# Router decisions from logits, a finer first gather, slot weights one batch at a time, and 28 unread products on TensorE

## The chip, the cores and the metric

The kernel runs on one core of one Trainium2 chip. The metric is the device time of one execution in microseconds (us). TensorE (PE; its weight loads are PEld) multiplies, VectorE (DVE) does elementwise work and reductions, ScalarE (ACT) evaluates functions and copies, GpSimd (POOL) helps, and SyncE (SP) issues the weight transfers on its DMA queue.

## The reference

One block of another kind comes first, then two layers of this form on 256 tokens of width 1024. The change concerns only the second half of each layer, a mixture of experts (MoE) with 4 groups of 8 experts:

```python
g_prob = softmax(t @ w_group + b_group)            # 4 groups
p_sel, g_idx = top_k(g_prob, 1)
e_in = the 8 expert logits of the chosen group
e_prob = softmax(e_in)
w_k, i_k = top_k(e_prob, 2);  w_k = w_k / sum(w_k)
combine = p_sel * one_hot(g_idx) * inner            # inner holds w_k at i_k
hid = silu(t @ w_gate[g]) * (t @ w_up[g]) * combine
x = x + sum over experts of hid @ w_down[g]
```

## The kernel before, in words

All matrices come from one packed array, in units of 1 MB (128 partitions x 2048 floats). `Stream` issues one transfer for each unit on SP's queue (L309) into a ring of buffers called `raw`; a unit's transfer is issued when the unit that held its buffer has been read. Before each MoE stage other pools are lent to the ring, so that it has 8 + 4 + 5 = 17 buffers.

The end of the mixers (`mixers2`) adds the output product to `x` for the token halves i = 0 and 1, and `r_logits` runs the router for a half in steps: sum of squares, transposes of `x` (`xT`, copied to `qh`), logits (`lg`, 8 products with 36 columns, then `L` on VectorE), the first group with the largest logit (`oh`), the chosen group's 8 logits (`el`), their largest (`emx`), an exponential on ScalarE with its sum (`pe`, `es`), a division, the two largest (`MAX` into `m8`, `MATCH_REPLACE`), the marks of the two chosen experts (`ci`), and `sel`, the 32 marks of a token. A product with a triangular matrix (`rank`) counts earlier tokens with the same expert, and `place` is the token's slot. `weave` and a list scheduler settle the order of the instructions; each engine then works its list strictly in order.

`route` compares `place` with the slot numbers: `OH[token, expert*32 + slot]` is 1 where the token sits. It makes the 256 columns of the first 8 experts (L1625, 128x256) and then the other 768, for each half. `gather` multiplies `x` by `OH` in row blocks k of 128 features: for a pair of batches (8 experts, 256 slots) and a k there are two products, one for each half i, and VectorE moves the result with a gain to `XT`. Before the change a step of `gather` handles two row blocks in one PSUM tile `gat`.

`experts` loops over NB = 8 batches of 4 experts. A batch has 8 units for gate and up (`gu`, one unit for each k: 4 products on 32 columns of the array) and 4 for down (`y`). After each unit `st.load()` lets SP issue the next transfer. `slots` multiplies all of `OH` by `ci` (`comb`, 16 products with 9 columns) for the weight and scale of every slot, and `tot` counts tokens for an overflow branch that is normally not taken. `turn_slots` transposes `OH` (`ohT`) for the way back (`sc`). All PE products have the helper's line L431.

The lines of the loop that set the order in the first batch:

```python
            for k in range(8):
                if b == 0 and k in (0, 2, 4):
                    next(first)
                w = unit()
                for j in range(4):
                    s.mm(q[j * SL:j * SL + SL, :], XT[b % 2][:, k, j * SL:j * SL + SL], w[:, j, :], k == 0, k == 7)
                st.load()
```

Of the kernel before, what the change touches and what calls it, by code (L numbers as in the profile page):

```python
# [16 lines left out]
T = 256  # L17
# [8 lines left out]
NB = 8  # L26
# [239 lines left out]
def run(*gens):  # L266
    for g in gens:
        for _ in g:
            pass
# [135 lines left out]
class KB:  # L405
# [754 lines left out]
    def mixers2(s, l, p):  # L1160
        nc, st = s.nc, s.st
        v = s.v = {}
        g = s.g("n2")[:, 8 * l:8 * l + 8]
        wr = s.g("router")[:, 288 * l:288 * l + 288].rearrange("p (k f) -> p k f", k=8)
        s.wr = s.p_ro.tile([128, 8, 36], F32, name="wr")
        nc.gpsimd.tensor_mul(s.wr, wr, g[:, :, None].to_broadcast([128, 8, 36]))
        for name, n in (("L", 36), ("r", 1), ("gt", 4), ("oh", 4), ("place", 32), ("psel", 1), ("ge", 4), ("gnx", 1), ("gmx", 2)):
            setattr(s, name, s.p_ro.tile([128, 2, n], F32, name=name))
        s.sel = s.p_ro.tile([128, 2, 32], F32, name="sel")
        s.ci = s.p_ro.tile([128, 2, 9], F32, name="ci")  # L1170
        xh = s.xnh = p.tile([128, 8, T], F32R, name="xnh")
# [24 lines left out]
        dense = s.m2_dense(l, pe)  # L1196
        weave((1.0, dense), (1.0, s.m2_stick(l, pe, dense)), (0.8, s.m2_mla(l, pe, (0, 1))))
        y = [[s.ps("wo", tag="y") for c in range(2)] for i in range(2)]
        m2 = s.m2_mla(l, pe, (2, 3))
        weave((1.0, s.m2_out(y, (6, 7, 4, 5))), (1.0, m2))  # L1200
        s.es_e.close()
        s.px = s.right(f"lx{l}")
        st.lend(s.px, "raw", s.E)
        U = [st.take() for k in range(4)]

        def last(i):
            for k in range(4):
                h, lo = U[k]
                mh, ml = s.m2_o(k)
                for c in range(2):  # L1210
                    s.mm3(y[i][c], mh[:, i * 128:i * 128 + 128], ml[:, i * 128:i * 128 + 128],
                          h[:, c * 512:c * 512 + 512], lo[:, c * 512:c * 512 + 512], False, k == 3)
                    yield 0.65

        run(last(0))
        weave((1.0, last(1)), (1.0, s.r_logits(l, p, 0, y[0])))
        st.done(4)
        st.lend(s.p_hl, "hl", s.S)
        run(s.r_logits(l, p, 1, y[1]))

    def right(s, name):

# [328 lines left out]
    def r_logits(s, l, p, i, y):  # L1551
# [27 lines left out]
        v.scalar_tensor_tensor(t, L[:, 0:4], mx[:, 0:1], s.c("first"), op0=OP.is_equal, op1=OP.mult)  # L1579
        v.tensor_reduce(mx[:, 1:2], t, axis=AX.X, op=OP.max)  # L1580
        v.tensor_scalar(oh, t, mx[:, 1:2], None, op0=OP.is_equal)

        v.tensor_scalar(s.gnx[:, i], mx[:, 0:1], -1.0, None, op0=OP.mult)
        nc.scalar.activation(s.ge[:, i], L[:, 0:4], AF.Exp, bias=s.gnx[:, i], accum_out=s.psel[:, i])
        yield 1.0


        def small(name, *shape):
            return s.p_ro.tile([128, *shape], F32, name=f"{name}{i}")

        em, el, emx, pe, es, m8, pr, w2 = (small(*n) for n in (("em", 4, 8), ("el", 8), ("emx", 1), ("pe", 16), ("es", 1), ("m8", 8), ("pr", 16), ("w2", 1)))
        v.tensor_mul(em, L[:, 4:36].rearrange("p (g e) -> p g e", g=4), oh[:, :, None].to_broadcast([128, 4, 8]))
        v.tensor_reduce(el, em.rearrange("p g e -> p e g"), axis=AX.X, op=OP.add)
        v.tensor_reduce(emx, el, axis=AX.X, op=OP.max, negate=True)
        nc.gpsimd.memset(pe, -1.0)
        nc.scalar.activation(pe[:, 0:8], el, AF.Exp, bias=emx, accum_out=es)
        yield 1.0
        v.reciprocal(es, es)
        v.tensor_scalar(pe[:, 0:8], pe[:, 0:8], es, None, op0=OP.mult)
        v.max(m8, pe[:, 0:8])  # L1600
        v.tensor_add(w2, m8[:, 0:1], m8[:, 1:2])
        v.memset(m8[:, 2:8], -1.0)
        v.match_replace(pr, m8, pe, -2.0)
        ci = s.ci[:, i]
        v.tensor_scalar(ci[:, 0:8], pr[:, 0:8], -2.0, None, op0=OP.is_equal)
        v.tensor_mul(s.sel[:, i].rearrange("p (g e) -> p g e", g=4), oh[:, :, None].to_broadcast([128, 4, 8]), ci[:, None, 0:8].to_broadcast([128, 4, 8]))
        yield 1.0

        q = s.ps("rank", tag="by"[i])
        s.mm(q[:, 0:32], s.c("lt"), s.sel[:, i], True, i == 0)  # L1610
# [4 lines left out]
        v.tensor_mul(w2, w2, s.psel[:, i])  # L1615
        v.reciprocal(w2, w2)
        v.scalar_tensor_tensor(ci[:, 0:8], ci[:, 0:8], w2, pe[:, 0:8], op0=OP.mult, op1=OP.mult)
        v.tensor_copy(ci[:, 8:9], s.r[:, i])

    def route(s, l, OH):  # L1620
        v = s.nc.vector
        for g0, g1 in ((0, 1), (1, 4)):
            for i in range(2):
                n = 8 * (g1 - g0)
                v.tensor_tensor(OH[:, i, g0 * 256:g1 * 256].rearrange("p (e s) -> p e s", s=SL), s.c("slot")[:, None, :].to_broadcast([128, n, SL]),  # L1625
                                s.place[:, i, g0 * 8:g1 * 8, None].to_broadcast([128, n, SL]), op=OP.is_equal)
        s.silu_set()

    def gather(s, l, XT, g, OH):

        gain = s.g("n2")[:, 8 * l:8 * l + 8]
        for k in range(0, 8, 2):
            q = s.ps("gat")
            for kk in range(2):
                d = slice((k + kk) * 128, (k + kk) * 128 + 128)
                for i in range(2):
                    s.mm(q[:, kk * 256:kk * 256 + 256], s.x[:, i, d], OH[:, i, g * 256:g * 256 + 256], kk == 0 and i == 0, i == 1)
            for j in range(2):
                s.nc.vector.tensor_tensor(XT[j][:, k:k + 2, :], q.rearrange("p (k j t) -> p k j t", k=2, j=2)[:, :, j], gain[:, k:k + 2, None].to_broadcast([128, 2, 128]), op=OP.mult)  # L1639
            yield  # L1640

    def slots(s, OH, comb):

        nc = s.nc
        v = nc.vector
        q = s.ps("comb")
        for b in range(NB):
            for i in range(2):
                s.mm(q[:, b * 9:b * 9 + 9], OH[:, i, b * 128:b * 128 + 128], s.ci[:, i, :], b == 0 and i == 0, i == 1)
        c9 = s.p_ro.tile([128, NB, 9], F32, name="c9")  # L1650
        v.tensor_copy(c9, q[:, :NB * 9].rearrange("p (b e) -> p b e", b=NB))
        c8 = c9[:, :, 0:8].rearrange("p (g h) e -> p g h e", h=2)
        v.tensor_mul(c8, c8, s.c("pick").rearrange("p (h e) -> p h e", h=2)[:, None].to_broadcast([128, 4, 2, 8]))
        v.tensor_reduce(comb[:, :, 0:1], c9[:, :, 0:8], axis=AX.X, op=OP.add)
        v.tensor_copy(comb[:, :, 1:2], c9[:, :, 8:9])
        v.tensor_mul(comb[:, :, 0:1], comb[:, :, 0:1], comb[:, :, 1:2])
        q = s.ps("tot")
        for i in range(2):
            s.mm(q[:, 0:32], s.one, s.sel[:, i], i == 0, i == 1)
# [13 lines left out]
    def experts(s, l, p, OH, OHT, comb):  # L1673
# [51 lines left out]
        for b in range(NB):  # L1725
# [1 line left out]
                es.enter_context(s.tc.manual_schedule(engines=_TAIL))  # L1727
            q = s.ps("gu")
            for k in range(8):
                if b == 0 and k in (0, 2, 4):  # L1730
                    next(first)
                w = unit()
                for j in range(4):
# [1 line left out]
                st.load()  # L1735
                if k == 1 and b:
                    hT = turned(hid)
                if k == 3:
                    if b == 0:
                        s.slots(OH, comb)  # L1740
                    if b % 2 == 0:
                        s.turn_slots(OH, OHT, b)
                    if b % 2 and b + 1 < NB:
                        nxt = tiles()
                        run(s.gather(l, nxt, b // 2 + 1, OH))
# [119 lines left out]
```

## Time and profile before

| | us |
|---|---|
| median of 3 runs (1229.9 to 1231.47) | 1230.11 |
| the profiled execution's own time | 1230.79 |
| its span, first to last instruction | 1229.0 |
| PE busy | 1112.7 (91%) |
| PEld / DVE / ACT / POOL busy | 824.7 / 566.2 / 462.6 / 127.9 |
| mean granted TensorE clock | 0.94 |

The profile divides the span into 40 slices of 30.7 us. The router and the start of the first MoE stage lie near 655 to 725 us, those of the second near 983 to 1040 us. A granted clock of 1.00 is 2.4 GHz and 0.50 is 1.2 GHz. A DMA share of 1.01 means that all 16 DMA engines were busy throughout.

### The profile page before, as it was taken

To read this page: it belongs to the slowest core of one execution; us is meant where nothing else is said; L and a number is where in the kernel's file an instruction comes from. 1 tells how busy PE (TensorE), PEld (TensorE's weight loads), DVE (VectorE), ACT (ScalarE), POOL (GpSimd) and SP (SyncE) were. 2 spreads that over 40 slices of the span, in tenths; PEclk is the share of its full clock that TensorE was granted. 3 is DMA by queue.
4 is the path that set the end of the run, shared out by engine and by line. 5 is a ranking of instruction groups with operands and counts; after the bars stand their busy time and mean duration, and the time that the engine had idled before them with its cause. 6 is when DMAs were issued, how large, how long until landed. Compare 5 with 4: busy or idle time off the path is not lost.

```text
span 1229.0 us, 18560 instructions
## 1 busy us (share of the span) xinstructions
PE 1112.7 (91%) x7474; PEld 824.7 (67%) x7474; DVE 566.2 (46%) x1121; ACT 462.6 (38%) x886; POOL 127.9 (10%) x143
## 2 busy tenths in 40 slices
PE   7999999999999999999998998867799989978665
PEld 7999999878789999998976623212198765313111
DVE  5555555669857555556865111100187552101002
ACT  6444444467646444445753010000177420110002
POOL 0222211000002221223120000000003000000000
PEclk9999999999999999999998899868889989988887
DMA  9754445653213545544428799999984389999996
GB/s 362 276 180 173 165 166 196 146 177 135 104 66 145 199 175 192 185 176 174 171 83 349 291 419 420 420 417 419 418 325 146 114 339 371 418 420 420 416 420 247
DMA packets 46469, 320.65 MB, mean 261 GB/s; under 512 B 5560, under 2 KB 5688, under 8 KB 9248
## 3 DMA queue, kind: packets, MB, share of 16 engines
q1 hardware_dynamic: 44640, 314.43, 65.0%
q0 software_dynamic: 1264, 4.26, 1.7%
q8 instruction: 62, 1.02, 0.3%
q10 hardware_dynamic: 464, 0.63, 0.1%
q14 instruction: 39, 0.32, 0.1%
HBM read 316.61 MB, written 2.69 MB: 260 GB/s over the span
## 4 chain that ended last, share of the span: by engine, by line
PE 67%; DMA 23%; DVE 6%; ACT 2%; issue 1%; SPq 0%; DVEq 0%; ACTq 0%
DMA raw<-in_weights_dram 22%; PE pg L431 11%; PE pu L431 10%; PE wo L431 6%; PE pd L431 5%; PE py L431 5%; PE gat L431 4%; PE gu L431 3%; PE sc L431 3%; PE qk L431 2%; PE y L431 2%; PE low L431 2%; PE po L431 2%; DVE whl L332 1%; PE qb L431 1%; PE iq L431 1%
## 5 line engine op out<-in xcount | busy, mean ns | idle before, releaser
L332 DVE TENSOR_TENSOR whl<-raw,whl 128x1024 fp32r<-128x1024 f32 (+2 forms) x211 | 261.1, 1239 | 153.7 <-ACT whl L331 153.6
L331 ACT CAST whl<-raw 128x1024 fp32r<-128x1024 f32 (+1 forms) x213 | 220.6, 1036 | 250.1 <-PE pu L431 53.1
L431 PE MATMUL gu<-raw,XT 128*32 128x512 f32 x1024 | 145.4, 670 | 42.1 <-DMA raw<-in_weights_dram 29.5
L431 PE MATMUL pg<-xh,whl 128*128 128x272 f32 (+1 forms) x704 | 137.5, 287 | 1.0 <-DVE gt L638 1.0
L431 PE MATMUL pu<-xh,whl 128*128 128x272 f32 (+1 forms) x704 | 136.2, 284 | 0.0
L431 PEld LDWEIGHTS pg<-xh,whl 128*128 128x128 f32 x704 | 113.1, 190 | 2.2 <-issue 1.2
L431 PEld LDWEIGHTS pu<-xh,whl 128*128 128x128 f32 x704 | 112.2, 188 | 0.0
L431 PEld LDWEIGHTS gu<-raw,XT 128*32 128x32 f32 x1024 | 26.2, 114 | 124.8 <-DMA raw<-in_weights_dram 67.7
L431 PE MATMUL pg<-xl,whl 128*128 128x272 f32 (+1 forms) x352 | 100.8, 286 | 0.0
L431 PE MATMUL pu<-xl,whl 128*128 128x272 f32 (+1 forms) x352 | 100.3, 285 | 0.0
L431 PE MATMUL y<-raw,hT 128*32 128x512 f32 x512 | 79.6, 707 | 17.3 <-DMA raw<-in_weights_dram 15.9
L1749 DVE SCALAR_TENSOR_TENSOR hid<-gu,comb,sg 128x256 f32<-128x256 f32 x16 | 7.7, 484 | 167.8 <-ACT sg L1747 167.8
L1747 ACT ACTIVATE sg<-gu,comb 128x256 f32<-128x256 f32 x16 | 7.6, 473 | 182.5 <-PE gu L431 182.5
L457 DVE TENSOR_TENSOR yl<-y,yh 128x512 fp32r<-128x512 f32 x32 | 22.1, 692 | 114.6 <-ACT yh L456 114.6
L431 PE MATMUL gat<-OH,x 128*128 128x256 f32 x256 | 71.1, 431 | 3.0 <-DVE OH L1625 3.0
L457 POOL TENSOR_TENSOR hl<-hid,hh 128x272 fp32r<-128x272 f32 (+1 forms) x44 | 57.7, 1310 | 123.8 <-ACT hh L456 123.7
L431 PEld LDWEIGHTS gat<-OH,x 128*128 128x128 f32 x256 | 52.8, 215 | 24.4 <-issue 11.7
L431 PEld LDWEIGHTS pg<-xl,whl 128*128 128x128 f32 x352 | 66.9, 190 | 0.8
L431 PE MATMUL pd<-hh,whl 128*128 128x272 f32 x352 | 66.9, 289 | 0.0
L431 PEld LDWEIGHTS pu<-xl,whl 128*128 128x128 f32 x352 | 66.2, 188 | 0.0
L456 ACT CAST yh<-y 128x512 fp32r<-128x512 f32 x32 | 18.7, 585 | 112.3 <-PE y L431 112.3
L1639 DVE TENSOR_TENSOR XT<-gat,sm 128x256 f32<-128x256 f32 x64 | 24.2, 420 | 76.7 <-PE gat L431 76.7
(413 smaller groups left out, 1984.8 us busy)
## 6 DMA issues: line engine op xcount, KB each, us to landing
raw<-in_weights_dram SPq DMA_DIRECT2D x290, 1024.0 KB, 15.4
raw<-in_weights_dram SPq DMA_DIRECT2D x6, 768.0 KB, 4.3
raw<-in_weights_dram SPq DMA_DIRECT2D x5, 512.0 KB, 7.6
dl<-line POOLq DMA_DIRECT2D x1, 1600.0 KB, 37.1
tb<-dl POOLq DMA_DIRECT2D x1, 1088.0 KB, 7.6
x<-in_x_dram SPq DMA_DIRECT2D x4, 256.0 KB, 5.0
c<-in_consts_dram POOLq DMA_DIRECT2D x1, 954.0 KB, 6.2
sm<-in_smalls_dram SPq DMA_DIRECT2D x1, 712.0 KB, 18.8
```

The lines of the kernel that those rows point to most:

```text
L331: s.kb.nc.scalar.copy(h[:, :n], raw)
L332: (s.kb.nc.gpsimd if s.spare is True or s.spare and j else s.kb.nc.vector).tensor_sub(l[:, :n], raw, h[:, :n].bitcast(F32))
L431: s.nc.tensor.matmul(out, l, r, start=start, stop=stop, skip_group_check=True)
L456: s.nc.scalar.copy(h, x)
L457: (s.nc.gpsimd if gpsimd else s.nc.vector).tensor_sub(l, x, h.bitcast(F32))
L1639: s.nc.vector.tensor_tensor(XT[j][:, k:k + 2, :], q.rearrange("p (k j t) -> p k j t", k=2, j=2)[:, :, j], gain[:, k:k + 2, None].to_broadc ...
L1747: nc.scalar.activation(sg, q[:, :256], AF.Silu, scale=comb[:, b, 1:2])
L1749: v.scalar_tensor_tensor(hid, q[:, 256:], comb[:, b, 0:1], sg, op0=OP.mult, op1=OP.mult)
```

## The change

Four things change in each of the two MoE layers. The two chosen experts are found from the logits `el` (padded to 16 with -3e38) and not from the exponentials; both exponentials of a half are issued later in the program, and a function `weights`, called in `route`, computes the weights of the chosen two. The first gather goes by single row blocks, one ahead of the loop and one before each `gu` of k = 0 to 6. `slots` runs for one batch at a time at k = 5, `turn_slots` at k = 5 of odd batches, and the count of tokens moves to batch 2 (`full`). Between the second half's logits and its `rank`, PE gets 28 products of 256 columns into a PSUM tile `idle` that nothing reads.

```diff
-        run(s.r_logits(l, p, 1, y[1]))
+        steps = s.r_logits(l, p, 1, y[1])
+        for n in range(4):
+            next(steps)
+
+        q = s.ps("idle")
+        for n in range(28):
+            s.mm(q[:, :T], s.ident_r, xh[:, 6, :])
+        run(steps)
...
-        nc.scalar.activation(s.ge[:, i], L[:, 0:4], AF.Exp, bias=s.gnx[:, i], accum_out=s.psel[:, i])
-        yield 1.0
...
-        v.tensor_reduce(el, em.rearrange("p g e -> p e g"), axis=AX.X, op=OP.add)
-        v.tensor_reduce(emx, el, axis=AX.X, op=OP.max, negate=True)
-        nc.gpsimd.memset(pe, -1.0)
-        nc.scalar.activation(pe[:, 0:8], el, AF.Exp, bias=emx, accum_out=es)
-        yield 1.0
-        v.reciprocal(es, es)
-        v.tensor_scalar(pe[:, 0:8], pe[:, 0:8], es, None, op0=OP.mult)
-        v.max(m8, pe[:, 0:8])
-        v.tensor_add(w2, m8[:, 0:1], m8[:, 1:2])
-        v.memset(m8[:, 2:8], -1.0)
-        v.match_replace(pr, m8, pe, -2.0)
+        v.tensor_reduce(el[:, 0:8], em.rearrange("p g e -> p e g"), axis=AX.X, op=OP.add)
+        v.max(m8, el[:, 0:8])
+        v.tensor_scalar(emx, m8[:, 0:1], -1.0, None, op0=OP.mult)
+        v.memset(m8[:, 2:8], -3.0e38)
+        v.match_replace(pr, m8, el, 3.0e38)
...
+        nc.scalar.activation(s.ge[:, i], L[:, 0:4], AF.Exp, bias=s.gnx[:, i], accum_out=s.psel[:, i])
+        nc.scalar.activation(pe, el[:, 0:8], AF.Exp, bias=emx, accum_out=es)
+
+        def weights():
+            v.reciprocal(es, es)
+            v.scalar_tensor_tensor(pe, pe, es, ci[:, 0:8], op0=OP.mult, op1=OP.mult)
+            v.tensor_reduce(w2, pe, axis=AX.X, op=OP.add)
+            v.tensor_mul(w2, w2, s.psel[:, i])
+            v.reciprocal(w2, w2)
+            v.tensor_scalar(ci[:, 0:8], pe, w2, None, op0=OP.mult)
+            v.tensor_copy(ci[:, 8:9], s.r[:, i])
...
         for g0, g1 in ((0, 1), (1, 4)):
+            if g0:
+                for f in s.weights:
+                    f()
...
-        for k in range(0, 8, 2):
+        n = 2 if g else 1
+        for k in range(0, 8, n):
...
-        for b in range(NB):
-            for i in range(2):
-                s.mm(q[:, b * 9:b * 9 + 9], OH[:, i, b * 128:b * 128 + 128], s.ci[:, i, :], b == 0 and i == 0, i == 1)
+        for i in range(2):
+            s.mm(q[:, 0:9], OH[:, i, b * 128:b * 128 + 128], s.ci[:, i, :], i == 0, i == 1)
...
-                if b == 0 and k in (0, 2, 4):
+                if b == 0 and k < 7:
                     next(first)
...
+                if k == 5:
+                    s.slots(OH, comb, b)
+                    if b % 2:
+                        s.turn_slots(OH, OHT, b - 1)
+                    if b == 2:
+                        s.full()
                 if k == 3:
-                    if b == 0:
-                        s.slots(OH, comb)
-                    if b % 2 == 0:
-                        s.turn_slots(OH, OHT, b)
```

On PE the list around the start of the first MoE stage (the second stage has the same) changes as follows; a space marks what stays, and 8 `gu` are two units.

```order
 L431 MATMUL lg<-wr,qh 128x36 x8
 L431 MATMUL rank<-sel,c_6164 128x32
-L431 MATMUL gat<-OH,x 128x256 x2
+L431 MATMUL idle<-xnh,ident_r 128x256 x28
 L431 MATMUL rank<-sel,c_6164 128x32
 L431 MATMUL rank<-sel,one 128x32
-L431 MATMUL gat<-OH,x 128x256 x6
-L431 MATMUL gu<-raw,XT 32x512 x8
 L431 MATMUL gat<-OH,x 128x256 x4
-L431 MATMUL gu<-raw,XT 32x512 x8
-L431 MATMUL comb<-ci,OH 128x9 x16
-L431 MATMUL tot<-sel,one 128x32 x2
```

The 28 products stand between the first half's `rank` and the second half's, four gather products now precede the first unit instead of eight, and the 16 `comb` products are no longer in front of the last two row blocks.

On VectorE, the list of before, from the first half's division to its search for the two largest (`r` and `L` are the second half's):

```order
L1598 RECIPROCAL es_7298<-es_7298 128x1
L479 SCALAR_TENSOR_TENSOR r<-rs_7351,rs_7350 128x1
L1599 TENSOR_SCALAR pe_7297<-pe_7297,es_7298 128x8
L1576 SCALAR_TENSOR_TENSOR L<-lg,r,sm 128x36
L1600 MAX m_7299<-pe_7297 128x8
```

The same place after the change, up to the first half's `sel`, which stood twelve rows below that MAX before:

```order
L1600 MAX m_7295<-el_7291 128x8
L1601 TENSOR_SCALAR emx_7292<-m_7295 128x1
L1602 MEMSET m_7295 128x6
L477 SCALAR_TENSOR_TENSOR rs_7344<-ss_7323,rs_7343 128x1
L1603 MATCH_REPLACE pr_7296<-m_7295,el_7291 128x16
L478 SCALAR_TENSOR_TENSOR rs_7344<-rs_7344,rs_7343 128x1
L1605 TENSOR_SCALAR ci<-pr_7296 128x8
L479 SCALAR_TENSOR_TENSOR r<-rs_7344,rs_7343 128x1
L1619 RECIPROCAL es_7294<-es_7294 128x1
L1606 TENSOR_TENSOR sel<-oh,ci 128x32
```

MAX no longer follows the division, but a RECIPROCAL of the exponential's sum, the first row of `weights`, now stands right ahead of `sel`.

Further down on VectorE, before, from the second half's `sel` to the first move out of the gather:

```order
L1606 TENSOR_TENSOR sel<-oh,ci 128x32
L1617 SCALAR_TENSOR_TENSOR ci<-ci,w_7380,pe_7376 128x8
L1613 SCALAR_TENSOR_TENSOR place<-rank,sel 128x32
L1625 TENSOR_TENSOR OH<-c_6164,place 128x256
L1625 TENSOR_TENSOR OH<-c_6164,place 128x768
L1639 TENSOR_TENSOR XT<-gat,sm 128x256 x6
```

And after the change, from the last row of the second half's `weights`:

```order
L1624 TENSOR_SCALAR ci<-pe_7368,w_7372 128x8
L1637 TENSOR_TENSOR OH<-c_6164,place 128x256
L1613 SCALAR_TENSOR_TENSOR place<-rank,sel 128x32
L1637 TENSOR_TENSOR OH<-c_6164,place 128x768
L1637 TENSOR_TENSOR OH<-c_6164,place 128x256
L1637 TENSOR_TENSOR OH<-c_6164,place 128x768
L1652 TENSOR_TENSOR XT<-gat,sm 128x128 x14
```

The first half's 768 columns moved from before the second half's `place` to between it and the second half's 256 columns.

## Rows read from the trace of the kernel before

**Rows 1.** The page: span, then forty equal slices (TensorE clock, DMA share).

```profile
span 1229.0 us, 18560 instructions
...
PEclk9999999999999999999998899868889989988887
DMA  9754445653213545544428799999984389999996
```

**Rows 2.** Chain that ended last, 650 to 740 us: start, us, what.

```profile
674.74 5.42 PE gat L431 x12
680.16 1.85 PE gu L431 x16
682.01 1.93 PE gat L431 x8
...
685.79 3.67 PE comb L431 x32
...
701.32 7.10 PE gat L431 x32
...
725.80 20.17 DMA raw<-in_weights_dram
```

**Rows 3.** Windows: stretch, length, busy PE PEld DVE ACT POOL, clock, DMA share, GB/s.

```profile
676.00:684.00 8.00, 8.00 (x38) 4.79 (x41) 1.54 (x5) 0.00 (x0) 0.00 (x0) 0.75 0.33 113
...
692.00:698.00 6.00, 6.00 (x45) 2.30 (x47) 0.80 (x3) 0.47 (x1) 0.76 (x3) 0.87 0.48 172
698.00:725.00 27.00, 26.31 (x176) 11.43 (x172) 5.33 (x12) 2.60 (x6) 0.00 (x0) 1.00 1.01 420
...
1004.00:1012.00 8.00, 8.00 (x40) 4.97 (x39) 1.59 (x5) 0.00 (x0) 0.00 (x0) 0.77 0.27 97
...
1020.00:1026.00 6.00, 6.00 (x46) 2.53 (x48) 0.76 (x2) 0.46 (x1) 0.00 (x0) 0.89 0.49 169
```

**Rows 4.** Waits of SP's queue, 670 to 700 us: total, times, longest.

```profile
SPq L309 <- PE gu L431: 30.3, 9, 16.4
```

**Rows 5.** Timeline of the second router: start, us, engine, line, out<-in, count, idle before.

```profile
994.83 0.16 DVE L1594 TENSOR_REDUCE emx<-el 128x1 f32<-128x8 f32 x1
...
995.50 0.16 DVE L1598 RECIPROCAL es<-es 128x1 f32<-128x1 f32 x1
996.23 0.26 DVE L1576 SCALAR_TENSOR_TENSOR L<-lg,r,sm 128x36 f32<-128x36 f32 x1 [0.30 <-DVE pe L1599]
997.39 0.19 DVE L1606 TENSOR_TENSOR sel<-oh,ci 128x32 f32<-128x32 f32 x1
997.63 0.63 PE L431 MATMUL rank<-sel,c 128*128 128x32 f32 x2 [1.93 <-DVE sel L1606]
...
998.94 0.95 DVE L1625 TENSOR_TENSOR OH<-c,place 128x768 f32<-128x768 f32 x1
1001.21 0.19 DVE L1606 TENSOR_TENSOR sel<-oh,ci 128x32 f32<-128x32 f32 x1
1002.56 0.19 DVE L1613 SCALAR_TENSOR_TENSOR place<-rank,sel 128x32 f32<-128x32 f32 x1 [0.89 <-PE rank L431]
1003.26 5.00 PE L431 MATMUL gat<-OH,x 128*128 128x256 f32 x12 [0.74 <-DVE OH L1625]
1008.19 1.92 PE L431 MATMUL gu<-raw,XT 128*32 128x512 f32 x16
```

**Rows 6.** Chain that ended last, 915 to 930 us: 256-column products of the idle kind.

```profile
920.94 5.69 PE qh L431 x48
```

**Rows 7.** Windows (columns as in rows 3) from the router on.

```profile
667.80:669.30 1.50, 0.00 (x0) 0.00 (x0) 1.50 (x19) 0.00 (x0) 0.00 (x0) 1.00 1.02 426
669.80:670.50 0.70, 0.02 (x1) 0.02 (x1) 0.70 (x5) 0.00 (x0) 0.00 (x0) 0.50 1.04 433
680.00:690.00 10.00, 10.00 (x79) 6.55 (x79) 1.78 (x6) 0.00 (x0) 0.00 (x0) 1.00 0.77 301
```

**Rows 8.** Groups by line over the whole span: busy, mean ns, idle before.

```profile
L1639 DVE TENSOR_TENSOR XT<-gat,sm 128x256 f32<-128x256 f32 x64 | 24.2, 420 | 76.7 <-PE gat L431 76.7
```

More of the change, by code (lines that the diff above doesn't have):

```diff
@@ L1170, in mixers2 @@
         s.ci = s.p_ro.tile([128, 2, 9], F32, name="ci")
+        s.weights = []
         xh = s.xnh = p.tile([128, 8, T], F32R, name="xnh")
@@ L1583, in r_logits @@
         v.tensor_scalar(s.gnx[:, i], mx[:, 0:1], -1.0, None, op0=OP.mult)
[L1584 to L1585 removed]
         def small(name, *shape):
             return s.p_ro.tile([128, *shape], F32, name=f"{name}{i}")
[L1591 removed]
+        em, el, emx, pe, es, m8, pr, w2 = (small(*n) for n in (("em", 4, 8), ("el", 16), ("emx", 1), ("pe", 8), ("es", 1), ("m8", 8), ("pr", 16), ("w2", 1)))
+        nc.gpsimd.memset(el, -3.0e38)
         v.tensor_mul(em, L[:, 4:36].rearrange("p (g e) -> p g e", g=4), oh[:, :, None].to_broadcast([128, 4, 8]))
[L1593 to L1603 removed]
+        v.tensor_reduce(el[:, 0:8], em.rearrange("p g e -> p e g"), axis=AX.X, op=OP.add)
[3 more added lines that the diff above has]
+        v.match_replace(pr, m8, el, 3.0e38)
         ci = s.ci[:, i]
[L1605 removed]
+        v.tensor_scalar(ci[:, 0:8], pr[:, 0:8], 3.0e38, None, op0=OP.is_equal)
         v.tensor_mul(s.sel[:, i].rearrange("p (g e) -> p g e", g=4), oh[:, :, None].to_broadcast([128, 4, 8]), ci[:, None, 0:8].to_broadcast([128, 4, 8]))
[L1607 removed]
+        yield 1.5
         q = s.ps("rank", tag="by"[i])
@@ L1613, in r_logits @@
         v.scalar_tensor_tensor(s.place[:, i], q[:, 0:32], 1.0, s.sel[:, i], op0=OP.add, op1=OP.mult)
[L1615 to L1618, printed above, removed]
+        nc.scalar.activation(s.ge[:, i], L[:, 0:4], AF.Exp, bias=s.gnx[:, i], accum_out=s.psel[:, i])
[8 more added lines that the diff above has]
+            v.tensor_copy(ci[:, 8:9], s.r[:, i])
+        s.weights.append(weights)
     def route(s, l, OH):
@@ L1631, in gather @@
         gain = s.g("n2")[:, 8 * l:8 * l + 8]
-        for k in range(0, 8, 2):
+        n = 2 if g else 1
+        for k in range(0, 8, n):
             q = s.ps("gat")
-            for kk in range(2):
+            for kk in range(n):
                 d = slice((k + kk) * 128, (k + kk) * 128 + 128)
@@ L1638, in gather, with slots, full @@
             for j in range(2):
-                s.nc.vector.tensor_tensor(XT[j][:, k:k + 2, :], q.rearrange("p (k j t) -> p k j t", k=2, j=2)[:, :, j], gain[:, k:k + 2, None].to_broadcast([128, 2, 128]), op=OP.mult)
+                s.nc.vector.tensor_tensor(XT[j][:, k:k + n, :], q[:, :n * 256].rearrange("p (k j t) -> p k j t", k=n, j=2)[:, :, j], gain[:, k:k + n, None].to_broadcast([128, n, 128]), op=OP.mult)
             yield
-    def slots(s, OH, comb):
-        nc = s.nc
-        v = nc.vector
+    def slots(s, OH, comb, b):
+        v = s.nc.vector
         q = s.ps("comb")
-        for b in range(NB):
-            for i in range(2):
-                s.mm(q[:, b * 9:b * 9 + 9], OH[:, i, b * 128:b * 128 + 128], s.ci[:, i, :], b == 0 and i == 0, i == 1)
[L1650 to L1656, printed above, removed]
+        for i in range(2):
+            s.mm(q[:, 0:9], OH[:, i, b * 128:b * 128 + 128], s.ci[:, i, :], i == 0, i == 1)
+        c8 = s.p_ro.tile([128, 8], F32, name="c8", bufs=2)
+        v.tensor_mul(c8, q[:, 0:8], s.c("pick")[:, b % 2 * 8:b % 2 * 8 + 8])
+        v.tensor_reduce(comb[:, b, 0:1], c8, axis=AX.X, op=OP.add)
+        v.tensor_copy(comb[:, b, 1:2], q[:, 8:9])
+        v.tensor_mul(comb[:, b, 0:1], comb[:, b, 0:1], comb[:, b, 1:2])
+    def full(s):
+        v = s.nc.vector
         q = s.ps("tot")
```

## The prediction

> **What bounds the kernel now.** I read the page first. TensorE is busy nearly throughout, but the slices of the DMA row show two plateaus at 9 behind the routers [rows 1]: there the weight stream sets the pace. The chain of waits says where each plateau begins. In the first MoE stage it runs through PE (gather, units, `comb`, again gather) until 725.80 and only then passes to weight transfers [rows 2]. So I cut the start of each stage into windows and read the DMA share. It is 1.01 when all engines are full; it is 0.33 over 676 to 684 us and 0.48 over 692 to 698, and in the second stage 0.27 over 1004 to 1012 and 0.49 over 1020 to 1026 [rows 3]. Idle transfer time is therefore 8 x (1 - 0.33/1.01) = 5.4 and 6 x (1 - 0.48/1.01) = 3.1 us in the first stage, 5.9 and 3.1 in the second: 17.5 us in all. Outside these holes the share is 1.01 to the stage's end, so this idle time is what the stage can give back, whatever the router itself costs. SP's queue names the cause: of 670 to 700 us it waited 30.3 for units to be read on PE [rows 4]. All 17 buffers were full, and the first hole lasts until PE has read the first unit. The second hole is the 3.67 us of `comb` and the two row blocks behind it [rows 2].
>
> What the change is worth thus hangs on when the first unit is read, and on whether PE then frees a buffer at least every 2.5 us (1.05 MB at 420 GB/s) [rows 3].
>
> **The router.** I take the second stage [rows 5]. MAX now stands where `emx` stood, at 994.83, and `emx` one step later, about 995.04 (a dependent step of VectorE costs about 0.2 here: 0.16 and the handover). Between `emx` and the RECIPROCAL lay 0.67 us, the exponential on ScalarE. The list still has a RECIPROCAL of that sum ahead of the first half's `sel`, so this wait is not removed: RECIPROCAL 995.71, `sel` about 995.85 instead of 997.39. The gain is 1.5 us, the division, the second `MAX` chain and the second half's rows that were interleaved. `rank` of the first half starts at about 996.05 and lasts 0.4 to 0.63.
>
> **The 28 products.** Queued behind them on PE is the second half's `rank`, and VectorE's `place` and PE's gather wait for that. In-kind products of 256 columns pass at 5.69/48 = 0.1185 us [rows 6], so 28 take 3.3 us and end near 999.8. The Trainium skill (TensorE: Matmul & The Clock Gate, section Back-to-back issue gap) gives an isolated 256-column product N/2.4 + 2.5 = 109 ns and says that this leaves out the weight load of a stream; by 109 ns they would end 0.26 us earlier and the sum below would be 0.5 us lower. The row is a stream with weight loads and decides.
>
> The second half's `sel` is ready before that: from `L` (996.23, unmoved) about fourteen dependent steps of 0.2 us, with `place` of the first half among them, put it near 999.1 instead of 1001.21. So the products cost 0.6 us on the path. Then `rank`, `place`: 1.1 us from `sel`'s end to `place` before at a clock of 0.50, about 0.7 at full clock, `place` near 1000.5. The `weights` rows of the second half (five between `sel` and `OH`, some 0.9 us) lie beside `rank`; without that cover they cost their 0.9.
>
> **The first gather.** Here something is lost: the first half's 768 columns (0.95 us) now stand between `place` and the second half's 256. From `place` to the gather it was 0.70 us; it becomes about 1.6, that is 1002.1. PE does the two first-half products meanwhile. Then two second-half products at 7.10/32 a record (two records each) [rows 2] take 0.9, the move to `XT` 0.2 to 0.42 (128 columns against 0.42 for 256 [rows 8]; I take 0.3, overlapping), and the first `gu` starts near 1003.2. It started at 1008.19: **5.0 us earlier**. Of that about 2.5 are the clock: before, twelve records took 5.00 us, 0.417 each, against 0.222 at full clock. The first stage has the same list and nearly the same times; with 680.16 as its first `gu` I take 4.8.
>
> **Behind the first unit.** A row block costs PE 1.93/2 = 0.97 for the gather and 1.85/2 = 0.93 for the unit, 1.9 us; VectorE needs at most 2 x 0.42 for it. Both are under 2.5, so transfers follow each other from the first unit on. The tightest place later is the second pair's gather, 7.10 us in one piece: units 0 to 11 with six row blocks, one `comb` and the turn take some 18 us, with that gather 25, and the twelfth buffer is due after 12 x 2.5 = 30. Hence the second holes (3.1 each) close. `comb` falls into eight pieces of 3.67/8 = 0.46 us, of which only one or two lie in the stretch that PE limits; the others and the moved `tot` and `ohT` lie where PE waits for weights. Without that cover they would cost the 4 us that they cost now.
>
> **Sum.** 4.8 + 3.1 + 5.0 + 3.1 = 16.0 us of 17.5. The rest of both stages is shifted, since the stream stays full to their ends and the second layer's mixers start when the first stage ends. Span 1229.0 - 16.0 = 1213.0. The profiled execution took 1230.79, 1.8 above its span, so 1214.8, and the median lies 0.7 below it: **1214.1 us**. Bounds of this case: all 17.5 gone, 1212.6; `OH` or the turn to `XT` slower by 1 us in each layer, 1216.
>
> **Rivals.**
> (a) *The clock falls before the 28 products.* The granted clock is 1.00 while PE has nothing for 1.5 us behind the logits products, and 0.50 soon after a short `rank` [rows 7]. Now only some 0.35 us are empty there, and full-width products follow; against it stands that the logits products, with 36 columns, precede. At 1.2 GHz the 28 take 3.3 x 0.417/0.222 = 6.2 us, to 1002.9; `rank` 1.1, four gather products 3.3, first `gu` about 1007.3, 0.9 earlier. The second holes still close: 4.0 a layer, 1222. Chance 9%.
> (b) *The second holes stay*, because PE, one block at a time, does not get ahead of the stream and the ring runs dry at the 7.10 us gather. My margin there is 5 us. 1214.1 + 6.2 = 1220.3. Chance 9%.
> (c) *The change does half of what it says*: the first stage's gain is used up before the second layer, by something other than the stream. Nothing in the windows shows such a wait. 1222. Chance 4%.
> (d) *The other side: alternating one block of gather with one unit brings the clock down.* A block at 1.2 GHz costs 4 x 0.417 + 2 x 0.93 = 3.5 us, more than 2.5. Over six blocks that opens 6.2 us of new idle, with the rest of the first hole about what there is now: level. It decides when the half clock lasts into the second pair's gather: that takes 13.3 instead of 7.10, the twelfth buffer comes at about 46 instead of 30, some 16 us of idle against 8.8 now, 7.5 more in each layer: 1245. Against it, gather and units alternated by pairs of blocks at 1.00 over 680 to 690 [rows 7]. The Trainium skill (the same page, section A second HAM failure mode) describes just this, short pauses between groups that cycle through PSUM banks and make the clock swing; in that window the trace does not agree. Chance 3% for level, 5% for slower.
>
> **How the numbers follow.** The forecast has 70%: both holes gone but for 0.6 to 0.9 us of the first. With (a) to (c) that makes 92% faster by over 0.2% (2.5 us, about what a measurement of this kernel can tell), 3% the same, 5% slower. The range takes in the forecast's own bounds and (a), (b) and (c): 1212.0 to 1222.5; what lies outside is (d) and surprises.
>
> **What would show it.** In the changed profile: first `gu` near 675 and 1003 if the routers begin where they do now; granted clock 1.00 through the `idle` products, which take 3.3 us; `sel` of the first half right behind RECIPROCAL; DMA share 1.01 within a microsecond of the first hole's beginning and no second hole; each batch's `comb` near half a microsecond; the plateaus shorter at their front and the same at their end. Wrong it would be if the clock reads 0.50 at the first gather, if the share falls again near 20 us behind the first `gu`, or if `rank` waits longer for the 28 products than VectorE needs for `sel` by more than a microsecond.

## The result and the profile after

The changed kernel took **1218.04 us** (median of 5 runs, 1216.11 to 1222.22) against 1230.36 (5 runs): a ratio of 0.9899, 95% interval 0.9878 to 0.9919. Two later comparisons of the same pair gave 0.9890 (0.9866 to 0.9913) and 0.9914 (0.9891 to 0.9937). So the change saves 10 to 12 us, where 16.0 was forecast; the span of the profiled execution is 1216.2 and not 1213.0.

Two rows of the page after, to be held against [rows 1] (TensorE's granted clock and the DMA share in 40 slices, now of 30.4 us):

```profile
PEclk9999999999999999999999999888789999989687
DMA  9744455652304555445426999999984389999995
```

In the first layer the slice that held the holes (669 to 699 us) now reads 9 and not 7; in the second the digits don't show the difference. The windows at the start of each stage (busy time of the engines, then clock, DMA share, GB/s), to be held against [rows 3]:

```profile
676.00:684.00 8.00, 8.00 (x52) 3.31 (x48) 1.70 (x9) 0.00 (x0) 0.00 (x0) 1.00 0.92 334
692.00:698.00 6.00, 6.00 (x39) 3.96 (x36) 0.77 (x3) 0.37 (x1) 0.00 (x0) 1.00 1.01 421
998.20:1006.00 7.80, 7.80 (x48) 3.12 (x47) 1.95 (x8) 0.00 (x0) 0.00 (x0) 1.00 0.92 332
1006.00:1012.00 6.00, 6.00 (x48) 2.44 (x50) 1.91 (x9) 0.47 (x1) 0.00 (x0) 1.00 1.01 425
1012.00:1026.00 14.00, 14.00 (x94) 8.31 (x90) 3.60 (x13) 0.96 (x2) 0.00 (x0) 1.00 1.01 420
```

The first hole is 8 x (1 - 0.92/1.01) = 0.7 us in each layer, and there is no second one. The timeline of PE through the second router, to be held against [rows 5]:

```profile
987.23 1.98 PE L431 MATMUL lg<-wr,qh 128*128 128x36 f32 x16
989.50 0.41 PE L431 MATMUL rank<-sel,c 128*128 128x32 f32 x2 [0.30 <-DVE sel L1606]
989.75 3.58 PE L431 MATMUL idle<-xnh,ident_r 128*128 128x256 f32 x28
993.16 0.31 PE L431 MATMUL rank<-sel,c 128*128 128x32 f32 x2
993.30 0.39 PE L431 MATMUL rank<-sel,one 128*128 128x32 f32 x2
993.91 1.13 PE L431 MATMUL gat<-OH,x 128*128 128x256 f32 x4 [0.23 <-DVE OH L1637]
995.21 1.13 PE L431 MATMUL gat<-OH,x 128*128 128x256 f32 x4 [0.17 <-DVE OH L1637]
996.30 1.07 PE L431 MATMUL gu<-raw,XT 128*32 128x512 f32 x8
997.29 1.13 PE L431 MATMUL gat<-OH,x 128*128 128x256 f32 x4
998.35 1.06 PE L431 MATMUL gu<-raw,XT 128*32 128x512 f32 x8
```

and of VectorE beside it:

```profile
989.21 0.15 DVE L1619 RECIPROCAL es<-es 128x1 f32<-128x1 f32 x1
989.28 0.17 DVE L1606 TENSOR_TENSOR sel<-oh,ci 128x32 f32<-128x32 f32 x1
...
992.33 0.19 DVE L1606 TENSOR_TENSOR sel<-oh,ci 128x32 f32<-128x32 f32 x1
...
993.44 0.42 DVE L1637 TENSOR_TENSOR OH<-c,place 128x256 f32<-128x256 f32 x1
993.77 0.18 DVE L1613 SCALAR_TENSOR_TENSOR place<-rank,sel 128x32 f32<-128x32 f32 x1
993.88 2.15 DVE L1637 TENSOR_TENSOR OH<-c,place 128x768 f32<-128x768 f32 x3
995.95 0.92 DVE L1652 TENSOR_TENSOR XT<-gat,sm 128x128 f32<-128x128 f32 x4
```

The second half's `sel` ends at 992.52 and its `rank` starts at 993.16, behind the last unread product: the products cost 0.6 us there. All three compares that are left stand between `place` and the first `XT`.

**How far the gain got.** The windows don't show where the rest of it went; the landings do. The table is worked out from the moment at which each transfer of SP's queue landed, counted from 0; a unit of a full stream lands every 2.49 us (1.05 MB). "Holes" adds up by how much the intervals of the first 23 units behind the router are over or under 2.494 us (units 114 to 136, and 222 to 244), "later" the same for the rest of the plateau (137 to 193, and 245 to 292). "Start" is the first logits product of layer 1; "first gu" and "stage" (landing of the stage's last unit, 193 and 300) are counted from the first logits product of the layer (the first half's). All in us, layer 1 / layer 2:

```
kernel            span    start   first gu      holes         later         stage
before            1229.0  661.68  18.41 18.55   9.60 10.51    1.25  0.33    227.70 226.77
changed           1216.2  662.49  13.16 13.15   2.07  1.92    1.55  2.49    220.49 219.87
e5_again          1220.6  665.48  13.16 13.16   1.77  2.03    2.31  2.40    220.93 220.23
e13_after_third   1217.8  664.99  13.17 13.17   1.68  2.58    1.56  1.71    220.12 219.70
e1_no_idle        1222.6  663.85  14.26 14.48   3.75  4.87    2.40  2.23    222.96 221.68
e2_router_only    1226.5  662.18  16.90 16.49   7.94 10.18    1.55  0.58    226.38 226.63
e3_fine_only      1221.2  661.17  15.16 15.04   5.10  5.75    1.81  1.95    223.86 222.35
e4_idle_only      1225.3  661.47  17.60 17.97   7.53  9.01    1.40  1.46    225.57 226.15
e9_shift          1218.2  664.07  13.16 13.17   2.07  1.64    2.05  2.44    220.55 219.41
e10_comb_whole    1215.1  661.47  13.18 13.16   4.03  4.11    0.98 -0.04    221.97 219.64
e11_early_none    1220.3  665.36  13.51 13.52   2.61  3.53    1.79  1.73    221.27 219.92
e8_early_gu       1214.2  662.98  12.10 12.09   0.57  0.22    1.74  2.11    219.10 218.03
e12_early_again   1213.1  661.84  12.10 12.09   0.76  0.24    1.67  1.94    219.19 217.84
```

In the changed kernel's first trace the stages are 7.2 and 6.9 us shorter, 14.1 in all. The first router started 0.8 later, the way from the last landing to the end is 0.6 longer, and the mixers between took 0.1 less: 12.8 us of span. Not all of what is left under "holes" is idle time: 0.98 of the 2.07 and 0.89 of the 1.92 are single intervals (units 122 and 226, landed at 704.26 and 1014.39 us) in stretches with a DMA share of 1.01, long intervals of a full stream like those under "later".

### The profile page after: what moved, and what is told of

Its sections match the earlier page's. It is cut to its first block, busy times and chain, and to the rows that moved or that the text cites. A ratio compares the mean times of both kernels' runs of the same rounds, so it can differ in the third digit from the quotient of the medians.

```text
span 1216.2 us, 18788 instructions
## 1 busy us (share of the span) xinstructions
PE 1104.3 (91%) x7530; PEld 823.7 (68%) x7530; DVE 574.1 (47%) x1191; ACT 463.1 (38%) x886; POOL 128.0 (11%) x143
## 3 DMA queue, kind: packets, MB, share of 16 engines
q8 instruction: 64, 1.05, 0.3%
## 5 line engine op out<-in xcount | busy, mean ns | idle before, releaser
L431 PE MATMUL y<-raw,hT 128*32 128x512 f32 x512 | 75.4, 676 | 16.6 <-DMA raw<-in_weights_dram 14.6
L431 PE MATMUL gat<-OH,x 128*128 128x256 f32 x256 | 63.9, 391 | 0.8 <-DVE OH L1637 0.8
L431 PEld LDWEIGHTS gat<-OH,x 128*128 128x128 f32 x256 | 45.9, 190 | 26.8 <-issue 18.4
L1652 DVE TENSOR_TENSOR XT<-gat,sm 128x256 f32<-128x256 f32 (+1 forms) x80 | 25.8, 366 | 73.7 <-PE gat L431 73.7
```

The source lines that it names most:

```text
L431: s.nc.tensor.matmul(out, l, r, start=start, stop=stop, skip_group_check=True)
L1652: s.nc.vector.tensor_tensor(XT[j][:, k:k + n, :], q[:, :n * 256].rearrange("p (k j t) -> p k j t", k=n, j=2)[:, :, j], gain[:, k:k + n, No ...
```

## The experiments

Theory: idle transfer time is the whole matter; the router, the products and the finer gather each shorten it, and whatever is closed in front reaches the end. Rivals: a part is worth nothing, or what is closed in front is lost behind.

**One part at a time.** e1 takes the products out of the changed kernel; e2, e3 and e4 put one part each into the kernel before.

```diff
# e1, on the changed kernel
-        steps = s.r_logits(l, p, 1, y[1])
...
-            s.mm(q[:, :T], s.ident_r, xh[:, 6, :])
-        run(steps)
+        run(s.r_logits(l, p, 1, y[1]))
# e2, on the kernel before: r_logits, weights and route of the change, nothing else
# e3, on the kernel before: gather, slots, full and the loop of experts of the change, nothing else
# e4, on the kernel before: the lines that e1 takes out
```

> The changed kernel without its 28 unread products. Theory: the granted clock falls to 0.50 behind the short rank, as it did before the change, and the first row blocks run at 1.2 GHz: 3.5 us a block instead of 2.06, above the 2.5 us of a transfer, so the first hole reopens by 1 us a block until the clock is back; first gu later by 0.5 to 1 us; together 2 to 4 us a layer, 1222 to 1226 us against 1218.0. Rival: the shorter router alone keeps the clock at 1.00 and the products buy nothing: 1216 to 1218, first gu 0.6 earlier.

> The kernel before with only the router by logits and the later weights; gather by pairs of row blocks, comb in one piece, no unread products. Theory: sel of the first half 1.5 us earlier and place of the second half 1.5 to 2 us earlier, less the 0.95 us of the 768 columns; first hole shorter by 1 to 2 us a layer, second holes stay, clock 0.50 at the first gather: 1226 to 1228. Rival: the time was set by the second half's logits anyway, and nothing is won: 1230.

> The kernel before with only the gather by single row blocks, comb by batches and the moved turn and count; router as before, no unread products. Theory: four instead of twelve records ahead of the first gu, 8 x 0.417 = 3.3 us earlier at the clock of 0.50; the second hole (3.1 us) closes, but blocks at 0.50 take 3.5 us until the clock is back, which gives 1 to 3 us of it back: 4 to 5.5 us a layer, 1219 to 1222. Rival: alternating at half clock takes all of it back: 1230.

> The kernel before with only the 28 unread products. Theory: they end before the second half's sel and cost nothing there; the first gather runs at 1.00, 12 records in 2.7 instead of 5.0 us, first gu 2.3 to 2.8 us earlier a layer, second holes stay: 1225 to 1226. Rival: the router of before is longer (sel of the second half at 1001.21), so that the clock falls again behind the products: 1230.

Measured against 1231.49 of the kernel before on that chip: e1 1224.65 (ratio 0.9937, 0.9912 to 0.9962), e2 1230.98 (0.9990, 0.9976 to 1.0004), e3 1223.18 (0.9935, 0.9914 to 0.9955), e4 1227.81 (0.9969, 0.9948 to 0.9990). e1 lies in its forecast; e2, e3 and e4 were some 3, 1.2 and 1.8 us slower than theirs. No part does it alone. e2, e3 and e4 save 0.5, 8.3 and 3.7 us, 12.5 together, which is about what the whole change saves. The router alone can't be told from no change, although its first `gu` comes 1.5 and 2.1 us earlier. The intervals of e1 and e3 overlap that of the whole change (0.9878 to 0.9919) a little; their stages in the table, 1.4 us or more longer in each layer than in any trace of the changed kernel, set them apart.

Windows of e1 over the first gather:

```profile
672.00:674.00 2.00, 0.50 (x3) 0.09 (x1) 1.85 (x11) 0.44 (x3) 0.00 (x0) 0.81 0.97 406
674.00:676.00 2.00, 1.06 (x4) 0.93 (x4) 1.16 (x9) 1.24 (x1) 0.00 (x0) 0.50 1.01 418
676.00:678.00 2.00, 1.90 (x4) 1.18 (x4) 1.61 (x6) 0.00 (x0) 0.00 (x0) 0.50 1.05 434
678.00:680.00 2.00, 2.00 (x10) 0.24 (x9) 0.49 (x2) 0.00 (x0) 0.00 (x0) 0.50 0.53 217
680.00:684.00 4.00, 4.00 (x28) 1.67 (x24) 0.98 (x4) 0.00 (x0) 0.00 (x0) 0.99 0.69 246
```

Without the products PE has 0.50 us of work in 2, the granted clock falls to 0.50, and row blocks at 1.2 GHz reopen the hole: shares of 0.53 and 0.69. Windows of e4, the products with the router of before:

```profile
668.00:670.00 2.00, 0.88 (x6) 0.89 (x7) 1.77 (x20) 0.39 (x2) 0.00 (x0) 0.89 1.03 422
670.00:672.00 2.00, 2.00 (x11) 2.00 (x11) 1.38 (x12) 1.68 (x3) 0.00 (x0) 0.50 1.00 414
672.00:674.00 2.00, 2.00 (x15) 2.00 (x15) 0.36 (x2) 0.00 (x0) 0.00 (x0) 0.76 1.01 422
```

Here the clock fell *before* the products. They began at 0.50 and the gather behind them had 1.00 again, but in layer 1 they took 5.07 us, and the second half's `rank` started 2.15 us after its `sel` had ended (674.27 and 672.12). The products hold the clock here only together with the shorter router: rival (a) of the prediction, seen in a part of the change but not in the whole.

**Chance or program.** e5 is the changed kernel unaltered. e9 adds, on it, 8 unread products of 32 columns behind each of the eight gate and up units of layer 1's third batch, which moves the places at which PE's later instructions are fetched.

```diff
                 st.load()
+                if l == 0 and b == 2:
+                    q2 = s.ps("shift")
+                    for _ in range(8):
+                        s.mm(q2[:, :32], s.ident_r, s.ident_r[:, :32])
```

> The changed kernel once more, unaltered, for its time beside the other runs and a second trace. In its first trace the weight stream of the plateaus lands a unit every 2.49 us but for single steps about 1 us longer (units 170, 181, 277 and 289 of SP's queue), which before had only at 170 and, 0.4 us long, at 277. If these steps belong to the program (where an engine's instructions are fetched), they come again at the same units, and the time is 1216 to 1219 us; if they are chance, they come elsewhere or not at all.

> The changed kernel with 64 unread products of 32 columns in the third batch of the first layer, where PE waits for weights: they move every later place at which PE's instructions are fetched (one packet of 16 KB for 256 of them) by half a packet. Theory that the long steps at units 181 and 289 come from PE's packets: they move to other units or vanish, 1216 to 1220 us. Rival, that they come from another engine's packets or from the order of the units: they stay at 181 and 289, 1218 us.

e5 took 1220.20, e9 1217.56 (0.9869, 0.9840 to 0.9898), beside 1232.56 of the kernel before. In e5 the long intervals came again at the same units or next to them (169, 181, 277, 288; 0.78 to 1.03 us over) with one at a new place (271, 0.86), so most of them belong to the program. In e9 the one at 181 became two of 0.29 and 0.55 at 180 and 181, and that at 289 stayed (0.96). For PE's own packets the trace decides at 289: queue 8, whose packets the insertion moved, had its last one 22.4 us ahead of that landing in e9 and 7.0 us in the changed kernel, and the interval stayed; a packet of queue 14 stood 2.7 and 3.6 us ahead. At 181 queue 8's was 6.0 and 17.2 us ahead, queue 14's 3.0 and 3.6. That is the rival of the text above.

**More instruction packets.** e6 runs 1500 memsets of one column on GpSimd in each layer.

```diff
         next(first)
+        tick = s.p_ro.tile([128, 1], F32, name="tick")
+        for k in range(1500):
+            nc.gpsimd.memset(tick, 0.0)
```

> The changed kernel with 1500 one-column memsets on GpSimd behind each router, 0.1 us each, which nothing reads and which end well before GpSimd has other work. They do no transfer, but their instructions have to be fetched, some twelve packets of 8 KB more in each plateau. Theory that such a packet holds up the unit that is due behind it by up to 1 us: more steps of the stream that are 0.3 to 1 us long, 1222 to 1240 us. Rival, that packets only take their bytes (12 x 8 KB at 420 GB/s are 0.2 us): 1218 us, no more long steps than before.

1261.8 us (1.0230, 1.0199 to 1.0262), more than either theory said, and for a third reason: the memsets wait for nothing, so many ran in the mixers (the first at 565.4 us) and held up GpSimd's work there (layer 1's router starts at 685.41). Its time says nothing of packets, but its plateaus do. The DMA queues of e6 over 1077 to 1218 us, of the changed kernel over 1032 to 1176 and of e10 (below) over 1032 to 1176 (queue, kind: packets, MB, share of 16 engines):

```profile
q8 instruction: 8, 0.13, 0.4%
q14 instruction: 12, 0.10, 0.2%
```

```profile
q8 instruction: 8, 0.13, 0.4%
q14 instruction: 8, 0.07, 0.1%
```

```profile
q8 instruction: 8, 0.13, 0.4%
q14 instruction: 6, 0.05, 0.1%
```

In the kernel before, 1046 to 1188 us, queue 14 had 4 packets. A packet of queue 14 in e6 is 8 KB and takes 0.31 us. Five of them, and the landings behind them, worked out from the packet and landing records:

```
packet at   next long landing   unit   interval (2.49 is usual)
1097.17     1098.60             242    3.16
1117.47     1119.21             250    3.14
1137.45     1139.79             258    3.14
1153.99     1155.41             264    3.14
1159.01     1161.06             266    3.15
```

The other seven of the twelve (1077.20, 1088.87, 1181.23, 1181.79, 1186.29, 1186.84, 1216.83) had no long interval behind them. In the changed kernel the long landings at 853.06 and 1174.34 stand 3.6 us behind such packets (849.43 and 1170.72). The bytes would be 0.02 us at 420 GB/s; what is lost is 0.65 to 0.98, and a stream without idle time didn't make it up.

Why some packets cost nothing can be read from the same traces. They keep 16 landing updates for each transfer; the table takes the last. Over the plateaus of all 14 traces, where no packet of queue 8 or 14 came from 10 us ahead of a unit's first update on (473 units), the 16 together shift against the usual interval by at most 0.13 us. Behind a packet that stands alone they shift by 1.39 to 1.71 us in sum for queue 8 (65 packets) and by 0.65 to 0.96 for queue 14 (16 packets). At units 181 and 289 of the changed kernel the last of the 16 alone moved, by 0.98, and the units behind kept it. So a packet acts as if it held up one sixteenth of the stream, and a unit's interval grows only when the part held up is the last or becomes it: by over 0.4 us behind 3 of the 65 and 7 of the 16. A share averaged over 16 engines doesn't show that.

The Trainium skill (Runtime: NRT & Kernel Launch, section Instruction fetch mechanics) says that sequencers fetch their instructions over DMA queues of their own in blocks of 16 KiB and that this is mostly hidden. Queue 8's packets here are 16 KB, queue 14's 8 KB. Whether an engine waited for its instructions no run here tells; from a saturated weight stream the cost isn't hidden.

**comb in one piece.** e10 is the changed kernel with `slots` of before, called once at k = 3 of batch 0.

```diff
                 if k == 5:
-                    s.slots(OH, comb, b)
...
                 if k == 3:
+                    if b == 0:
+                        s.slots(OH, comb)
```

> The changed kernel with comb in one piece again, where it stood before (at k = 3 of the first batch, behind the third unit). Theory that the second hole was comb's 3.67 us: by then three units are under way, 7.5 us of transfers, and the next buffer comes free 4.1 + 2.06 + 3.67 = 9.8 us behind the first; 2.3 us of idle transfer time a layer, 1222 to 1223 us, DMA share below 0.8 in a window of some 8 us there. Rival, that the finer gather alone closes the second hole: 1218 to 1219.

1220.26 us (0.9916, 0.9895 to 0.9937), the same as the changed kernel beside it (1220.19, 0.9914). The hole is back, as the windows of e10 show (the second is the one behind `comb`, where the granted clock fell too):

```profile
676.00:678.00 2.00, 2.00 (x13) 0.80 (x12) 0.49 (x2) 0.00 (x0) 0.00 (x0) 1.00 0.74 258
...
688.00:692.00 4.00, 4.00 (x20) 2.01 (x16) 0.49 (x2) 0.00 (x0) 0.00 (x0) 0.75 0.72 254
```

The table has it at 4.0 and 4.1 us instead of about 2. But "later" fell to 0.98 and -0.04, and the second stage is as long as in the changed kernel (219.64), the first 1.5 us longer than its mean. The hole has the size that was forecast (2.2 and 1.9 us over the mean of the changed kernel's traces), but the total has not, and neither theory had this: the hole was comb's, yet by this one trace closing it buys nothing in the second layer and part of its size in the first.

**VectorE's list put right.** e8 lets both compares of 768 columns and the `weights` rows wait, by a false dependence, for the first blocks of `XT`, and has 14 products; e11 is e8 without products; e12 is e8 again, e13 the changed kernel again.

```diff
-        for n in range(28):
+        for n in range(14):
...
-        def weights():
+        def weights(X):
+            v.scalar_tensor_tensor(es, X[:, 0:1], 0.0, es, op0=OP.mult, op1=OP.add)
...
+    def others(s, OH, i, X):
+        v = s.nc.vector
+        slot = s.p_ro.tile([128, SL], F32, name="slot2", bufs=2)
+        v.scalar_tensor_tensor(slot, X[:, 0:SL], 0.0, s.c("slot"), op0=OP.mult, op1=OP.add)
+        v.tensor_tensor(OH[:, i, 256:1024].rearrange("p (e s) -> p e s", s=SL), slot[:, None, :].to_broadcast([128, 24, SL]),
+                        s.place[:, i, 8:32, None].to_broadcast([128, 24, SL]), op=OP.is_equal)
...
+                if b == 0 and k in (0, 2):
+                    s.others(OH, k // 2, XT[0][:, k + 1, :])
+                if b == 0 and k == 1:
+                    for f in s.weights:
+                        f(XT[0][:, 2, :])
```

> The changed kernel with VectorE's list put right by dependences: the weights rows and both compares of 768 columns stand behind the first row blocks of XT instead of ahead of them, and 14 unread products instead of 28. Theory: second half's place 1.5 us earlier, first gu 2 to 2.7 us earlier in each layer, but only 0.6 to 0.7 us of transfer time is still idle there, so the gain is at most 1.3 us: 1216.5 to 1217.5. Rival: with 14 products the clock falls before the gather ends, and blocks of 3.5 us reopen the hole: 1220 to 1224.

> The kernel with VectorE's list put right, without any unread products. Theory: even the shorter way to the gather leaves PE with little behind the logits products, the clock falls to 0.50 before the gather ends, and a hole of 1.5 to 3 us opens in each layer: 1221 to 1224 us. Rival: the pause is now too short for the clock to fall, and the products can go: 1217 to 1218, clock 1.00 throughout 664 to 684.

> The kernel with VectorE's list put right and 14 products, again, beside the changed kernel on one chip. Its holes were gone (DMA share 0.99 to 1.04 in each 2 us of 668 to 684). Theory: 1 to 1.5 us faster than the changed kernel, 0.9987 of its time. Rival: the two are the same within the spread of runs.

> The changed kernel, unaltered, on the same chip as the run beside it: 1217 to 1221 us. First gu 13.16 us behind the second half's first logits product in both layers, as in its two earlier traces; the mixers ahead of it, whose length differed by 3 us between those two, decide the rest.

e8 1218.37 (0.9873, 0.9847 to 0.9899) beside e5's 1220.20; e12 **1215.12** (0.9871, 0.9851 to 0.9892) beside e13's 1220.19; e11 1222.03 (0.9929, 0.9905 to 0.9953). (The text on e13 counts its 13.16 us from the second half's logits product; they run from the first half's, as in the table.) The first `gu` comes only 1.1 us earlier, not 2 to 2.7, and yet both stages shrink, by 1.4 and 2.0 us against the mean of the changed kernel's three traces. The list and the 14 products weren't tried apart: in layer 1 of e8 `rank` starts 0.4 us earlier, since it no longer waits for products, and the list gives the rest of the 1.1. Windows of e12:

```profile
676.00:678.00 2.00, 2.00 (x13) 0.83 (x12) 1.90 (x16) 0.00 (x0) 0.00 (x0) 1.00 1.03 410
678.00:680.00 2.00, 2.00 (x13) 0.83 (x12) 1.67 (x5) 0.00 (x0) 0.00 (x0) 1.00 0.99 385
680.00:684.00 4.00, 4.00 (x25) 1.67 (x24) 0.98 (x4) 0.00 (x0) 0.00 (x0) 1.00 1.01 416
684.00:692.00 8.00, 8.00 (x68) 2.84 (x66) 1.98 (x9) 0.85 (x2) 0.00 (x0) 1.00 1.01 422
```

No hole is left. The bound of 1.3 us, taken from the share of 0.92, was too low, since the landings had 2 us under "holes" in each layer, the intervals at 122 and 226 among them, and e8 and e12 have no long interval there. e12 has the lowest median of all versions, and its four executions are below all six of e13; but each of the two intervals overlaps that of the changed kernel beside it, and e12's trace also starts layer 1 3.2 us earlier than e13's. So the times alone don't settle the step; the stages in the traces do. e11 shows that even here the products are needed: 1.4 us at the first `gu`, holes of 2.6 and 3.5.

## Why the prediction was nearly right

**Bound and cause: right.** The idle transfer time in the four holes bounds the gain, and the first unit's reading ends the first of them. By the windows 17.5 us became 1.4, so 16.1 were closed, where the sum had 16.0; by the landings 20.1 became 4.0, again 16.1. The time is less right than that: 1218.04 lies outside the forecast's own bounds (1212.6 to 1216), and in the range only because the range takes in rivals (a) to (c), none of which happened in the changed kernel.

**First `gu`: right.** 5.25 and 5.4 us earlier in the table, forecast 4.8 and 5.0. Step by step, with the second layer's logits products 6.5 us earlier than before (the second half's at 987.23): the second half's `place` was forecast for 1000.5, that is 994.0, and came at 993.77; the first `gu` for 996.7, and came at 996.30; `sel` right behind RECIPROCAL; 0.6 us of waiting for the products. The products took 3.58 and not 3.3 us, 0.128 each; the Trainium skill's 109 ns for an isolated one (TensorE: Matmul & The Clock Gate, section Back-to-back issue gap) is still further off.

**"Of that about 2.5 are the clock": wrong share of a right sum.** The twelve records that it was priced on give 12 x (0.417 - 0.222) = 2.3, and the finer gather leaves four ahead of the first unit: in layer 1 of e1 they take 2.08 us, with the products 1.13. The products as a whole are worth 1.1 and 1.3 us at the first `gu` by e1, and that isn't the clock alone: without them the list scheduler puts the first half's compares (0.41 and 0.95 us) ahead of the second half's `sel` again, which ends 1.0 us later, while the 0.6 us of waiting for products is gone. The holes are 1.9 and 2.7 us larger in e1 than the mean of the changed kernel's traces; what the later first `gu` doesn't account for lies in the blocks.

**Second holes: right that they close.** A block takes 2.05 us (996.30 to 998.35), forecast 1.9, below the 2.49 of a transfer, at a clock of 1.00. So the alternation of gather and units did not swing the clock, as rival (d) would have had it. The pauses between groups of which the Trainium skill (the same page, section A second HAM failure mode) speaks were not there: PE was busy 8.00 of 8 us over 676 to 684, and 10.00 of 10 in the prediction's window [rows 7], so neither tests that section.

**The step that was mis-sized: "The rest of both stages is shifted, since the stream stays full to their ends."** The stream did stay full, but a full stream isn't a constant one. The stages shrank by 7.2 and 6.8 us (mean of three traces) where 7.9 and 8.1 were summed. In the second layer the intervals behind unit 244 exceed the usual ones by 0.33 us before and by 1.7 to 2.5 in all three traces of the changed kernel; e10, with `comb` in one piece, has -0.04. So "`comb` falls into eight pieces" was charged nothing behind the first units, and by e10 it gives back there all that it wins in front in the second layer. The packets say how. The nine traces with `comb` in pieces and without e6's memsets have a packet of queue 14 1.8 to 3.6 us ahead of unit 181, with 0.55 to 0.98 us lost there, and six packets of queue 14 between the landings of units 244 and 292; the four with `comb` in one piece have no such packet and no long interval at 181, and five packets behind 244. The one packet more stands 1.5 to 3.6 us ahead of a long interval (0.72 to 1.03) at 288 or 289 in six of the nine, and at 283 (e11) and 279 (e8, e12) where the packet had moved. That is 0.6 to 1.0 us in each layer. It isn't the only cause: e4 has `comb` in one piece too, and 1.46, of which 1.10 stand 2.3 us behind a packet of queue 8; and the intervals at 276 to 278, where packets of both queues crowd in all kernels, are longer in the changed kernel for a reason that stays open. The other part of the shortfall, 0.8 to 3.8 us ahead of the first router, lies where the change does nothing: PE, VectorE and ScalarE have the same lists up to there as before (last section).

Rivals (b) and (c) fell: the share stays at 1.01 where (b) has its hole, and (c) looks for the loss outside the stream, where the mixers between the stages differ by 0.1 us in the first trace; the loss in the stages lies in the stream.

## What to carry to other kernels

When a transfer stream is the bound, sum the idle time in front of it, but test the shift behind it by the landings of single units: a share of 1.01 hid intervals that were 1 us too long here. More instructions on another engine lengthened the stream here, since their packets came in between. Parts that each work on one pause can depend on each other: the unread products kept the clock with the shorter router and not with the longer one. Look in the list of each engine, not only in the code, for rows (compares, weights) that stand ahead of the first thing that is waited for.

## What the runs showed that was not expected

Executions of one kernel differ by steps of some 1.5 us in mixers that the change doesn't touch. Windows of the third trace of the changed kernel (e13):

```profile
232.00:238.00 6.00, 6.00 (x30) 5.34 (x30) 1.76 (x3) 1.04 (x4) 0.00 (x0) 0.72 0.66 125
625.00:631.00 6.00, 5.70 (x39) 5.03 (x38) 1.81 (x4) 1.33 (x3) 0.21 (x1) 0.72 0.07 29
```

and of its first:

```profile
232.00:238.00 6.00, 6.00 (x40) 4.99 (x40) 2.61 (x4) 2.46 (x6) 0.00 (x0) 1.00 0.63 113
625.00:631.00 6.00, 6.00 (x55) 5.22 (x55) 2.22 (x3) 3.22 (x6) 0.00 (x0) 1.00 0.00 0
```

The granted clock dipped (to 0.50 within these windows) in e5, e11 and e13 at both places, and in e1, e2 and e9 at the second alone. Ahead of the second place PE had waited 2.2 us for ScalarE, in traces with the dip and without. Each of the two dips goes with a shift of about 1.5 us: layer 1's first logits product starts at 664.99 to 665.48 with both, at 662.18 to 664.07 with one, at 661.17 to 662.98 with neither. A third dip, near 567 us, stands in seven of these thirteen traces and goes with some 0.5 us. The two may be much of the spread of the changed kernel's runs (1216 to 1224); it was seen in profiled executions only.
